# An encoder trunk on one core: elementwise work behind the first stage moves from GpSimd to VectorE

## The chip, the cores and the metric

One core of a Trainium2 chip runs the whole program. The metric is the device time of one execution in microseconds, the median over several runs. The core has five engines with queues of their own that work side by side and signal each other by semaphores: TensorE (PE in the profile; its weight loads are PEld), VectorE (DVE), ScalarE (ACT), GpSimd (POOL) and SyncE (SP, which here only issues loads and stores).

## The reference

A trunk of two layers over 256 tokens of width 2048, all in float32. Layer 0 mixes tokens with a bidirectional S5 state-space model and a gated linear unit, layer 1 with windowed grouped-query attention; each is followed by an MLP with a squared ReLU, 8192 wide.

```python
for i in range(DEPTH):                      # DEPTH = 2
    if i % 2 == 0:
        h = h + s5_mixer(rms_norm(h, s5_norm[j]), ...)      # ends: (z @ w_glu_a) * sigmoid(z @ w_glu_b)
    else:
        h = h + windowed_gqa(rms_norm(h, attn_norm[j]), positions, ...)
    h = h + sqrelu_mlp(rms_norm(h, mlp_norm[i]), mlp_w_up[i], mlp_w_down[i])

# windowed_gqa: 32 query heads, 4 key heads of 64; q and k get a norm per head and a rotation
x1, x2 = x[..., :half], x[..., half:]
concatenate([x1 * cos - x2 * sin, x2 * cos + x1 * sin])
# softmax over |i-j| <= 128 with a sink logit per head, then @ w_o
# sqrelu_mlp: square(relu(h @ w_up)) @ w_down
```

## The kernel before

**Precision.** Each factor of a large product is held as a rounded high part (fp32r) and the rest, its low part, and three products are summed: high by high, low by high, high by low (`mm3`, lines 717 to 719; the MLP has its own forms at lines 858, 860 and 924). So every weight tile must be split before TensorE can use it.

**Weights.** `wload` fetches the next tile of a fixed list, `wsrc`: a load on SP's queue into a ring of raw buffers (line 674), a copy on ScalarE that rounds to the high part (line 679), a subtraction that gives the low part (line 680). A table `whow` says for a tile into how many pieces these two are cut and which engine subtracts: "v" is one whole tile of 128x2048 on VectorE, "vv" two halves there, "g" one whole tile on GpSimd, "gggg" four quarters there. The constant `QH` gives this for the 20 tiles of the attention's projections (four for keys and values, then four for each of the four groups of heads), `UH` for the first five tiles of the first up projection, `OH` for the output projection. Every other tile is "v", apart from those of the first stage that a range `WP` gives to GpSimd, and those of the down projection that `wload_fast` splits (lines 693 to 698).

**Stages, in order of time.** The S5 stage with tables, scan and output, beside which the gated unit's first half runs (to some 290 us; GpSimd works through most of it). The rest of the gated unit (`glu_rest`, to some 394 us): per block of 512 columns and half of the tokens, `glu_post` multiplies by the sigmoid, adds to the residual (lines 816 to 823) and calls `norm_pre`, which multiplies the residual by the norm's gain (line 735) and squares it on ScalarE; `norm_post` transposes that product on TensorE and splits it (lines 744 to 747). Then the first MLP (up projection to 751 us, down projection to some 1097 us), whose end takes four norm products for attention through `scaled`. Then attention: keys and values, then four groups of eight heads each, whose projection by TensorE is set between the softmax steps of the group before. Per group and half of the tokens: `head_r` makes the head norms (lines 1095 to 1101, with the reciprocal square root at lines 199 to 208), `rope` the rotation by two products and a sum (lines 1086 to 1088), then come scores with a running maximum (line 1134), exponentials on ScalarE (line 1149), the division (line 1153), transposes (1159) and the product with the values (1168). Keys go through `rope` too, and two copies on GpSimd (line 1230). The output projection ends with residual sums and norm products for the second MLP (`fin`, line 1267), to some 1389 us. The second MLP is like the first, without norm products.

**Order.** Each engine takes its instructions in the order of its own queue. That order is not the order of the source: the program is built with `TileContext(nc, schedule_with_timeline_sim=True)`, which plans the queues by a simulated timeline. A few orders are fixed by hand with `issue_after`. The attention's steps are set between TensorE's tiles by the table `HS`.

Of the kernel before, what the change touches and what calls it, by code (L numbers as in the profile page):

```python
# [35 lines left out]
WP = range(9, 33)  # L36
WD = 20 + 16 + 64 + 64
FAST = (range(2, 27, 3), (0, 4, 7, 10, 13, 16, 20, 23, 26))
QH = ("v", "vv", "vv", "v") + ("vv", "g") * 8
UH = ("vv", "vv", "gggg", "vv", "vv")  # L40
OH = ("v",) * 16


# [134 lines left out]
class Kernel:  # L178
# [549 lines left out]
        self.nc.sync.dma_start(gain, self.gain_src[:, cb * 512:(cb + 1) * 512])  # L728
        return gain

    def norm_pre(self, cb, tt, gain, hg, e=None):

        nc = self.nc
        r = self.resid[:, tt, cb * 512:(cb + 1) * 512]
        (e or nc.gpsimd).tensor_mul(hg, r, gain)
        sq = self.tmp.tile([P, 512], F32, name="sq")
        nc.scalar.activation(sq, r, AF.Square, accum_out=self.ss[:, tt, cb:cb + 1])

# [105 lines left out]
    def mlp(self, nxt, fin):  # L844
        nc, ar = self.nc, self.ar
# [53 lines left out]
        v = nc.vector  # L899
        aform, atail = [], []  # L900

        def split(kp, fast, own=False):
            h = hTs[0][:, 2 * kp:2 * kp + 2] if kp < 16 else hTs[kp // 8 - 1][:, kp % 8 * 2:kp % 8 * 2 + 2]
            h = h.rearrange("p k c -> p (k c)")
            a = (atail if own else aform)[kp % 2]
            n = a.shape[1] // 2
            if fast:
                s = pool.tile([P, 7 * P], F32, name="sr", bufs=1)
                q = h.rearrange("p (x c) -> p x c", x=4)
                t = s.rearrange("p (x c) -> p x c", x=7)  # L910
                nc.scalar.copy(s[:, :3 * P], h[:, P:])
                v.tensor_add(t[:, 3:5], q[:, 1:4:2], q[:, 0:1].broadcast_to([P, 2, P]))
                v.tensor_add(t[:, 5], t[:, 4], q[:, 1])
                v.tensor_add(t[:, 6], t[:, 5], q[:, 2])
                h = s
            c = h.shape[1]
            nc.scalar.copy(a[:, :c], h)  # L917
            v.tensor_sub(a[:, n:n + c], h, a[:, :c].bitcast(F32))  # L918
            return a[:, :n], a[:, n:]
# [14 lines left out]
        def fast(a, w, first, end):  # L934
            for bk, j, g, c in LATE if first else FORMS:
                mm(bk, a, j, w[g], c, stop=end and bk[0] != "x")

        def plain(a, w, bk, stop=False):
            t, j = divmod(bk, 2)
            bk = "x%d" % (bk + 1)  # L940
            for i in range(2):
                mm(bk, a, (1, 0, 2, 3)[2 * i + t], w, (2, 3)[i] if j == 0 else i, stop=stop and i == 1)
# [4 lines left out]
        def fold():  # L947
            c, d, u, w = (self.tmp.tile([P, 512], F32, name=n) for n in ("hg", "hg", "sq", "gain"))
            g = nc.gpsimd
            nc.scalar.copy(c, bks["p1"])  # L950
            g.dma_start(rs(0, 0), c, accum_op=ALU.add)  # L951
            v.tensor_sub(u, c, bks["q6"])
            v.tensor_sub(w, u, bks["q5"])
            g.dma_start(rs(0, 1), w, accum_op=ALU.add)
            v.tensor_sub(u, bks["q7"], u)
            g.dma_start(rs(1, 0), u, accum_op=ALU.add)
            v.tensor_add(d, u, bks["q5"])
            g.dma_start(rs(1, 1), d, accum_op=ALU.add)

        def end(half, t, j):  # L960
            cb = half * 2 + j
            cs = slice(cb * 512, (cb + 1) * 512)
            v.tensor_add(self.resid[:, t, cs], self.resid[:, t, cs], bks["x%d" % (2 * t + j + 1)])
            if last:
                nc.sync.dma_start(self.d["out"][:, t, cs], self.resid[:, t, cs])
            elif half:
                scaled(t, cb, nc.gpsimd)
                if j:
                    self.norm_end(t)

        def scaled(t, cb, e):
            self.norm_pre(cb, t, gains[:, cb * 512:(cb + 1) * 512], hx[:, t, cb], e)

        atail += [ar.get("at#%d" % i, [1024], F32R, at=49664 + 1024 * i) for i in range(2)]
        nx = split(0, False, True)
# [7 lines left out]
        for half in range(2):  # L983
            bks, begun = {}, set()
            pend = []
            for kp in range(NK):
                a = nx
                if half == 0 and kp == 2:
                    ar.free("at")
                    self.wr[0].add(ar.get("wx#49664", [2048], at=49664))  # L990
                if half and kp == NK - 4:
                    for r in self.wr:
                        r.drop()
                    ar.free("wx")
                    atail[:] = [ar.get("at#%d" % i, [1024], F32R, at=49664 + 1024 * i) for i in range(2)]
                if kp + 1 < NK:
                    nx = split(kp + 1, kp + 1 in FAST[half], kp == 0 if not half else kp + 1 >= NK - 2)
                elif not half:
                    nx = split(0, 0 in FAST[1])
                w = self.wnext() if half or kp else w0  # L1000
                if half and kp == 19 and not last:
                    ar.free("hT#0")
                    hx = ar.get("hx", [2, 4, 512], at=31744)
                    gains = ar.get("hg", [D], at=35840)
                    nc.sync.dma_start(gains, self.d["gains"][nxt])
                    self.ss = self.small.tile([P, 2, 4], F32, name="ss")
                    for t in range(2):
                        for cb in range(2):
                            scaled(t, cb, v)
                if kp in FAST[half]:  # L1010
                    fast(a, w, not begun, kp == FAST[half][-1])
                    if kp == FAST[half][-1]:
                        fold()
                elif kp < NK - 1 - half:
                    for b in range(4):
                        plain(a, w, b)
                else:
                    pend.append((a, w))
            if half:
                ar.free("hT", "af")  # L1020
                if not last:
                    self.act = ar.get("act", [KT, 2, L], F32R, at=23552)
            n = half and not last
            for t in range(2):
                for p in pend[:n]:
                    for j in range(2):
                        plain(*p, 2 * t + j)
                for j in range(2):
                    for p in pend[n:]:
                        plain(*p, 2 * t + j, stop=p is pend[-1])  # L1030
                    end(half, t, j)
# [46 lines left out]
    def rope(self, pool, src, n, x, tt):  # L1078

        v = self.nc.vector  # L1080
        t1 = pool.tile([P, n, 2, 32], F32, name="rp_a") if n == 8 else self.tmp.tile([P, n, 2, 32], F32, name="gain")
        t2 = pool.tile([P, n, 2, 32], F32, name="rp_b", bufs=1) if n == 8 else self.tmp.tile([P, n, 2, 32], F32, name="sq")
        sv = src.rearrange("p (n s c) -> p n s c", n=n, s=2)
        A = self.ropeA[:, x, tt].rearrange("p (o s c) -> p o s c", o=1, s=2).broadcast_to([P, n, 2, 32])
        B = self.ropeB[:, x, tt].rearrange("p (o s c) -> p o s c", o=1, s=2).broadcast_to([P, n, 2, 32])
        v.tensor_mul(t1, sv, A)
        v.tensor_mul(t2, sv[:, :, ::-1], B)
        self.nc.gpsimd.tensor_add(t1, t1, t2)
        return t1.rearrange("p n s c -> p (n s c)")

    def head_r(self, pool, src, n, tt, scale, name):
# [194 lines left out]
    def run(self):  # L1286
        nc, d, ar = self.nc, self.d, self.ar
        self.wq = []
        self.whow = {**{163 - j: h for j, h in enumerate(QH)}, **{143 - j: h for j, h in enumerate(OH)}, **{291 - j: h for j, h in enumerate(UH)}}
        self.wsrc = ([d["wge"][c, k] for c in (1, 2, 3, 0) for k in range(KT // 2)] + [None] + [d["wgl"][c, k] for c in range(4) for k in range(KT // 4)]  # L1290
# [219 lines left out]
```

## Time and profile before

| | us |
|---|---|
| median of three runs (lowest, highest) | 2092.61 (2088.96, 2093.38) |
| the profiled execution | 2089.93 |
| its span, first to last instruction | 2088.1 |
| busy: TensorE, VectorE, ScalarE, GpSimd | 2013.2, 1476.5, 1091.0, 338.5 |

In the profile's rows a name as L680 is a line of the kernel, `slot` is any buffer of the big arena, `bank` any of the eight banks in which TensorE leaves results. A shape as 128x512 is partitions by elements of each. A wait is named by the line that waited and by what released it last.

### The profile page before, as it was taken

The numbers are of one execution on the slowest core, as the hardware profiler recorded it, in microseconds if no ns is written. First come the engines' busy times: TensorE is split into PE (matmuls) and PEld (weight loads), VectorE is DVE, ScalarE is ACT, GpSimd is POOL, SyncE is SP. The second block draws the span as 40 slices with busy tenths as digits, with TensorE's granted clock in tenths as the row PEclk, the third lists the DMA queues.
The fourth block names the chain that finished last, engine by engine and source line by source line (L and its number), as shares of the span: only waits on it lengthen the run. The fifth ranks groups of instructions, "written<-read, shape, count | busy, mean of one in ns | idle before, by whom it ended". The sixth has DMA issues, their size and how long they took to land.

```text
span 2088.1 us, 33141 instructions
## 1 busy us (share of the span) xinstructions
PE 2013.2 (96%) x13736; PEld 1693.2 (81%) x13736; DVE 1476.5 (71%) x2096; ACT 1091.0 (52%) x1314; POOL 338.5 (16%) x260
## 2 busy tenths in 40 slices
PE   5989999899999999999999889999999999999999
PEld 4877778788888888878787667888888888787887
DVE  8899636755555578988886877465555557898886
ACT  5553645444444455655554556454444445565553
POOL 6988721200000000000022430100000000000000
PEclk9999999999999999999999999999999999999999
DMA  3224455455555555465564332455555555547554
GB/s 120 71 98 145 153 194 200 166 197 187 196 182 193 191 196 207 181 222 207 198 206 172 121 121 81 149 186 200 193 190 184 197 185 198 204 182 241 182 205 158
DMA packets 61990, 368.47 MB, mean 176 GB/s; under 512 B 7072, under 2 KB 9408, under 8 KB 21904
## 3 DMA queue, kind: packets, MB, share of 16 engines
q1 hardware_dynamic: 54144, 342.32, 46.0%
q10 hardware_dynamic: 5184, 19.49, 2.7%
q0 software_dynamic: 2512, 4.56, 1.2%
q8 instruction: 107, 1.75, 0.3%
q14 instruction: 43, 0.35, 0.0%
HBM read 360.05 MB, written 2.10 MB: 173 GB/s over the span
## 4 chain that ended last, share of the span: by engine, by line
PE 62%; DVE 9%; DMA 7%; ACT 3%; issue 2%; POOL 0%; SPq 0%; ACTq 0%; DVEq 0%
PE bank L858 22%; PE bank L924 22%; PE bank L860 12%; DMA slot<-in_wdn 4%; DVE slot L680 4%; PE bank L717 2%; PE bank L718 1%; PE bank L719 1%; ACT slot L679 1%; DVE slot L694 1%; ACT slot L693 1%; DMA slot<-in_wup 1%; DMA slot<-in_wo 1%; ACT slot L1149 1%; PE bank L1168 1%
## 5 line engine op out<-in xcount | busy, mean ns | idle before, releaser
L680 DVE TENSOR_TENSOR slot<-slot,slot 128x2048 fp32r<-128x2048 f32 (+1 forms) x285 | 628.8, 2209 | 417.2 <-ACT slot L679 414.6
L679 ACT CAST slot<-slot 128x2048 fp32r<-128x2048 f32 (+2 forms) x321 | 554.6, 1733 | 466.5 <-PE bank L858 195.1
L924 PE MATMUL bank<-slot,slot 128*128 128x512 f32 x2124 | 493.4, 390 | 2.5 <-DVE slot L918 1.8
L858 PE MATMUL bank<-slot,slot 128*128 128x512 f32 x2048 | 492.4, 392 | 2.8 <-DVE slot L747 1.6
L924 PEld LDWEIGHTS bank<-slot,slot 128*128 128x128 f32 x2124 | 397.7, 188 | 88.4 <-DVE slot L918 4.2
L858 PEld LDWEIGHTS bank<-slot,slot 128*128 128x128 f32 x2048 | 377.0, 189 | 76.5 <-DVE slot L747 2.2
L860 PEld LDWEIGHTS bank<-slot,slot 128*128 128x128 f32 x2048 | 263.1, 191 | 10.3
L860 PE MATMUL bank<-slot,slot 128*128 128x256 f32 x2048 | 266.3, 283 | 0.0
L717 PE MATMUL bank<-slot,slot 128*128 128x512 f32 x544 | 219.2, 404 | 5.2 <-ACT slot L679 4.9
L719 PE MATMUL bank<-slot,slot 128*128 128x512 f32 x544 | 209.5, 398 | 7.3 <-POOL slot L680 7.1
L718 PE MATMUL bank<-slot,slot 128*128 128x512 f32 x544 | 215.5, 396 | 0.0
L924 PE MATMUL bank<-slot 128*128 128x512 f32 x840 | 201.1, 391 | 4.1 <-DVE slot L918 3.4
L951 POOL DMA_DIRECT2D slot<-slot x4 | 3.7, 921 | 1159.0 <-ACT slot L950 1149.3
L924 PEld LDWEIGHTS bank<-slot 128*128 128x128 f32 x840 | 157.0, 188 | 40.2 <-DVE slot L918 6.5
L694 DVE TENSOR_TENSOR slot<-slot,slot 128x1536 fp32r<-128x1536 f32 x72 | 145.5, 2021 | 39.5 <-ACT slot L693 36.4
L693 ACT CAST slot<-slot 128x1536 fp32r<-128x1536 f32 x72 | 122.3, 1698 | 93.3 <-DMA slot<-in_wdn 46.5
L869 ACT ACTIVATE slot<-slot 128x256 f32<-128x256 f32 x128 | 52.8, 414 | 159.0 <-DVE slot L867 159.0
L717 PEld LDWEIGHTS bank<-slot,slot 128*128 128x128 f32 x544 | 104.0, 191 | 30.0 <-ACT slot L679 6.1
L719 PEld LDWEIGHTS bank<-slot,slot 128*128 128x128 f32 x544 | 102.8, 191 | 31.4 <-POOL slot L680 9.1
L718 PEld LDWEIGHTS bank<-slot,slot 128*128 128x128 f32 x544 | 103.9, 191 | 20.8 <-issue 0.7
L917 ACT CAST slot<-slot 128x512 fp32r<-128x512 f32 (+1 forms) x128 | 90.5, 709 | 53.5 <-PE bank L924 52.9
L680 POOL TENSOR_TENSOR slot<-slot,slot 128x1024 fp32r<-128x1024 f32 (+2 forms) x36 | 100.6, 2808 | 104.6 <-ACT slot L679 98.9
(238 smaller groups left out, 1800.0 us busy)
## 6 DMA issues: line engine op xcount, KB each, us to landing
slot<-in_wup SPq DMA_DIRECT2D x128, 1024.0 KB, 4.9
slot<-in_wdn SPq DMA_DIRECT2D x128, 1024.0 KB, 4.9
slot<-in_wqkv SPq DMA_DIRECT2D x20, 1024.0 KB, 5.0
slot<-in_wge ACTq DMA_DIRECT2D x32, 512.0 KB, 3.8
slot<-in_wgl SPq DMA_DIRECT2D x16, 1024.0 KB, 5.3
slot<-in_wo SPq DMA_DIRECT2D x16, 1024.0 KB, 4.9
slot<-in_bz SPq DMA_DIRECT2D x16, 336.0 KB, 3.3
slot<-in_cp SPq DMA_DIRECT2D x16, 256.0 KB, 2.7
```

The lines of the kernel that those rows point to most:

```text
L679: self.nc.scalar.copy(hi[:, c], raw[:, c])
L680: (self.nc.gpsimd if e == "g" else self.nc.vector).tensor_sub(lo[:, c], raw[:, c], hi[:, c].bitcast(F32))
L693: self.nc.scalar.copy(hi, x)
L694: v.tensor_sub(lo, x, hi.bitcast(F32))
L717: pe.matmul(out, lhsT=xh, rhs=wh, start=first, stop=False)
L718: pe.matmul(out, lhsT=xl, rhs=wh, start=False, stop=False)
L719: pe.matmul(out, lhsT=xh, rhs=wl, start=False, stop=last)
L858: pe.matmul(bk, lhsT=wh[:, kt], rhs=act[:, kt].rearrange("p x c -> p (x c)"), start=(kt == 0), stop=False)
L860: pe.matmul(bk[:, :L], lhsT=wl[:, kt], rhs=act[:, kt, 0], start=False, stop=(kt == KT - 1))
L869: nc.scalar.activation(o if fb % 2 else o[:, ::-1], s.rearrange("p (x c) -> p x c", x=2), AF.Square)
L917: nc.scalar.copy(a[:, :c], h)
L924: pe.matmul(bank(bk), lhsT=a[x][:, j], rhs=w[y][:, c], start=bk not in begun, stop=stop and y == 1)
```

## The change

Three things that GpSimd does behind the first stage are done by VectorE:

- the low parts of weights: eight tiles of the heads' projections, which were whole tiles on GpSimd, become whole tiles on VectorE (`QH`); the third tile of the first up projection goes from four quarters on GpSimd to two halves on VectorE, and its rounding copies on ScalarE from four to two (`UH`);
- the products of residual and gain in `norm_pre`: eight in the gated unit, four at the end of the first down projection (`end`, second half) and eight in attention's `fin`; the four that `scaled` does in the middle of the down projection were VectorE's before;
- the sum that ends a rotation in `rope`: eight for the heads, two for the keys.

GpSimd keeps the first stage's work, the key copies of line 1230 and the DMAs that it issues.

```diff
-QH = ("v", "vv", "vv", "v") + ("vv", "g") * 8
-UH = ("vv", "vv", "gggg", "vv", "vv")
+QH = ("v", "vv", "vv", "v") + ("vv", "v") * 8
+UH = ("vv", "vv", "vv", "vv", "vv")
...
-    def norm_pre(self, cb, tt, gain, hg, e=None):
+    def norm_pre(self, cb, tt, gain, hg):
...
-        (e or nc.gpsimd).tensor_mul(hg, r, gain)
+        nc.vector.tensor_mul(hg, r, gain)
...
             elif half:
-                scaled(t, cb, nc.gpsimd)
+                scaled(t, cb)
...
-        def scaled(t, cb, e):
-            self.norm_pre(cb, t, gains[:, cb * 512:(cb + 1) * 512], hx[:, t, cb], e)
+        def scaled(t, cb):
+            self.norm_pre(cb, t, gains[:, cb * 512:(cb + 1) * 512], hx[:, t, cb])
...
-                            scaled(t, cb, v)
+                            scaled(t, cb)
...
-        self.nc.gpsimd.tensor_add(t1, t1, t2)
+        v.tensor_add(t1, t1, t2)
```

## The prediction

> **What bounds the kernel now.** I read the page's head first, then the sums by stretch, then TensorE's own waits, then the chain of waits in the stretches where TensorE stands still, and last the timeline of GpSimd beside that chain.
>
> ```profile
> span 2088.1 us, 33141 instructions
> PE 2013.2 (96%) x13736; PEld 1693.2 (81%) x13736; DVE 1476.5 (71%) x2096; ACT 1091.0 (52%) x1314; POOL 338.5 (16%) x260
> ```
>
> TensorE is busy for 96% of the span, so a change on other engines can only win where TensorE is not fed. The next view says where that is (per engine: busy us and number of instructions; then the granted TensorE clock, the DMA share and GB/s).
>
> ```profile
> core 0: us, PE busy (x) PEld busy (x) DVE busy (x) ACT busy (x) POOL busy (x), PEclk, DMA share, GB/s
> 345.00:400.00 55.00, 50.87 (x236) 41.73 (x235) 40.01 (x51) 27.33 (x37) 18.03 (x10) 0.97 0.50 177
> 1040.00:1100.00 60.00, 60.00 (x282) 50.01 (x281) 49.84 (x85) 35.73 (x42) 11.40 (x13) 1.00 0.57 182
> 1130.00:1180.00 50.00, 43.23 (x201) 33.37 (x201) 38.39 (x93) 22.04 (x39) 21.44 (x10) 0.93 0.33 118
> 1180.00:1230.00 50.00, 42.32 (x258) 31.80 (x256) 37.85 (x102) 30.33 (x62) 17.98 (x5) 0.94 0.33 126
> 1230.00:1280.00 50.00, 47.37 (x278) 36.33 (x276) 37.57 (x117) 28.89 (x66) 12.70 (x5) 0.92 0.30 106
> 1335.00:1400.00 65.00, 63.79 (x315) 53.32 (x314) 37.87 (x50) 31.08 (x34) 11.11 (x7) 1.00 0.49 170
> 1400.00:1742.00 342.00, 342.00 (x1971) 302.43 (x1970) 190.85 (x191) 161.45 (x190) 0.00 (x0) 1.00 0.55 192
> ```
>
> Behind the first stage GpSimd works in just the stretches where TensorE idles. In 1130 to 1280, the heads of attention, TensorE idles 6.8 + 7.7 + 2.6 = 17.1 us of 150, and its granted clock there is 0.93, 0.94 and 0.92: 7%, 6% and 8% of 50 us, 10.5 us of lost speed at most. At the turn from the gated unit to the first up projection (345 to 400) it idles 4.1 us at clock 0.97, 1.7 us more. Between 1400 and 1742 it is busy for 342.00 us of 342: what is saved earlier is not waited away there. So at most 17.1 + 10.5 + 4.1 + 1.7 + 1.2 (1335 to 1400), some 35 us, can be won.
>
> What ends TensorE's waits, in 1100 to 1400 and then in 300 to 410 (total, times, longest):
>
> ```profile
> PE bank L1168 <- DVE mx L1134: 4.7, 1, 4.7
> PE bank L719 <- POOL slot L680: 4.1, 3, 2.0
> PE bank L1159 <- DVE slot L1153: 4.0, 2, 2.5
> PE bank L717 <- ACT slot L679: 3.5, 1, 3.5
> ```
>
> ```profile
> PE bank L744 <- POOL slot L735: 3.9, 1, 3.9
> ```
>
> Two of the five name GpSimd (a weight subtraction, a norm product), two VectorE's softmax, one the scalar engine's weight copy. Why VectorE is late is in the chain of waits (start, length, piece): its longest pieces between 1118 and 1225, set beside two rows of GpSimd's timeline:
>
> ```profile
> 1119.64 3.58 DVE hms L1098
> 1133.55 5.59 DVE slot L680
> 1139.16 4.99 DMA slot<-in_wqkv
> 1150.83 4.46 DVE rs_h L200
> ...
> 1184.81 1.92 DVE slot L1153 x7
> 1189.65 3.72 DVE slot L680
> 1193.81 6.81 DMA slot<-in_wqkv
> 1204.01 4.30 DVE slot L680
> 1217.53 6.47 DVE slot L1153 x8
> ```
>
> ```profile
> 1118.57 4.62 POOL L680 TENSOR_TENSOR slot<-slot,slot 128x2048 fp32r<-128x2048 f32 x1 [22.50 <-ACT slot L679]
> ```
>
> ```profile
> 1150.67 4.58 POOL L680 TENSOR_TENSOR slot<-slot,slot 128x2048 fp32r<-128x2048 f32 x1
> ```
>
> L1098 and L200 work on a few numbers per partition, yet take 3.58 and 4.46 us. They end at 1123.22 and 1155.29; GpSimd's subtractions end at 1123.19 and 1155.25. VectorE stood still until GpSimd was done. Undisturbed, the same forms take (groups by shape of 1180 to 1230 and 1230 to 1285; count, busy us, mean ns):
>
> ```profile
> L200 DVE TENSOR_SCALAR rs_h<-hms 128x8 f32<-128x8 f32 x2 | 0.3, 161 | 0.0
> ```
>
> ```profile
> L680 DVE TENSOR_TENSOR slot<-slot,slot 128x1024 fp32r<-128x1024 f32 x1 | 1.2, 1216 | 0.0
> ```
>
> Seven instructions of L1153 take 1.92 us in the chain's own row at 1184.81, 0.27 each; the eight at 1217.53 take 6.47.
>
> So the chain holds stalls of 3.4 (L1098, taken at L200's 0.16), 5.59 - 1.22 = 4.4, 4.46 - 0.16 = 4.3, 3.72 - 1.22 = 2.5, 4.30 - 1.22 = 3.1 and 6.47 - 8 x 0.27 = 4.3: 22.0 us in which the chain waits for GpSimd without naming it.
>
> **The change part by part.** The durations, by groups of one shape: GpSimd's costliest of 300 to 1400, then VectorE's two nearest.
>
> ```profile
> L680 POOL TENSOR_TENSOR slot<-slot,slot 128x2048 fp32r<-128x2048 f32 x8 | 38.5, 4811 | 66.2 <-ACT slot L679 66.2
> L735 POOL TENSOR_TENSOR slot<-slot 128x512 f32<-128x512 f32 x16 | 28.0, 1757 | 173.2 <-DVE slot L1267 62.9 <-issue 58.3 <-DVE slot L823 33.3
> L1088 POOL TENSOR_TENSOR slot<-slot,slot 128x512 f32<-128x512 f32 x8 | 15.2, 1900 | 48.6 <-DVE slot L1087 28.0 <-DVE hms L1098 17.1 <-DVE slot L208 2.5
> L735 POOL TENSOR_TENSOR slot<-slot,slot 128x512 f32<-128x512 f32 x4 | 5.1, 1290 | 16.1 <-DVE slot L963 16.0
> L680 POOL TENSOR_TENSOR slot<-slot,slot 128x512 fp32r<-128x512 f32 x4 | 5.0, 1291 | 8.2 <-ACT slot L679 8.2
> ```
>
> ```profile
> L680 DVE TENSOR_TENSOR slot<-slot,slot 128x2048 fp32r<-128x2048 f32 x249 | 571.3, 2296 | 400.8 <-ACT slot L679 400.5
> ```
>
> ```profile
> L735 DVE TENSOR_TENSOR slot<-slot,slot 128x512 f32<-128x512 f32 x4 | 2.5, 684 | 0.0
> ```
>
> *The heads' weights (QH).* Eight of the projection's tiles change from "g" to "v": GpSimd loses 8 x 4.81 = 38.5 us, VectorE gains 8 x 2.30 = 18.4. By code a tile is still one copy on the scalar engine, one subtraction and one load on SP's queue; the next load into its raw buffer, and what stands behind it on SP's queue, waits for the subtraction, now in VectorE's queue. The chain shows what that wait is worth: a 4.99 us load starts at 1139.16, as a stalled subtraction ends, a 6.81 us load at 1193.81 behind another. *The rotation sums (L1088).* Eight of 128x512 and two of half that go to VectorE. It shows no sum of this form with four dimensions; the nearest row is its own 128x512 product from two buffers, 0.68 us, the farthest GpSimd's own 1.90. I take 0.68, since that row is of the same engine and size: 8 x 0.68 + 2 x 0.34 = 6.1 (bounds 0, if they fit into idle time, and 17.1). Moved work in attention: 18.4 + 6.1 = 24.5 us, against 22.0 us of stalls on the chain alone. VectorE's load is about the same; but what was a 4.6 us block at any moment becomes 2.3 us in queue order, and the tile is ready 2.5 us sooner.
>
> What TensorE gets of it. The three waits for L680 on GpSimd, 4.1 us, go: the subtraction is half as long, and VectorE idles some 12 us of each 50 there. Bounds: all 4.1, or none if the tile queues for 2 us behind other VectorE work; I take 4.1. The 4.7 us wait at L1168 stands behind the 6.47 us run of L1153, which held a 4.3 us stall; the subtraction that made it now stands somewhere in VectorE's queue for 2.3: I take 4.3 - 2.3 = 2.0 (bounds 0 and 4.7). The other two, 4.0 + 3.5, end in the softmax: VectorE's stalls ahead of them go, the moved work comes, and the scalar engine's exponentials between remain. I take half, 3.7 (bounds a loss of 2.5, 24.5 - 22.0, and a gain of 7.5). Together 9.8 of the 16.3 us in these four rows, or 60%. What is late next there is the exponentials.
>
> The clock falls with the waits. I take the same 60% of 10.5: 6.3 us (bounds 0 and 10.5). In 1230 to 1280 the longest wait in the rows is the 2.5 us of L1159, and the clock is 0.92 all the same: waits that are only shortened to some 2 us can still cost it. The Trainium skill ("TensorE: Matmul & The Clock Gate", What's actually happening) puts the fall to half speed behind at least one idle window of about 3.4 us; what that would make of the sum is rival 4, and the 2.5 us wait beside 0.92 speaks against it.
>
> *The turn into the up projection (UH, norm products of the gated unit).* Tile 2's subtractions go from four of 1.29 on GpSimd to two of 1.22 on VectorE, its copies from four to two. Eight products of L735 follow, of 20 in all. Timeline rows:
>
> ```profile
> 389.86 1.68 DVE L822 TENSOR_TENSOR slot<-slot,slot 128x512 f32<-128x512 f32 x1
> ```
>
> ```profile
> 392.35 1.77 POOL L735 TENSOR_TENSOR slot<-slot 128x512 f32<-128x512 f32 x1 [1.35 <-DVE slot L823]
> ```
>
> L822 is 1.0 over the 0.68 of its size and ends with GpSimd's subtraction; the product, on the chain, goes from 1.77 to 0.68, 1.1 less. Against these 2.1 us stand up to 2.4 of subtractions ahead of the chain. VectorE idles 15 us of this stretch of 55, so I take half, 1.2: a gain of 0.9 (bounds a loss of 2.4 and a gain of 5.8, all idle time and clock).
>
> *The other twelve products.* Four at the end of the first down projection lie where TensorE is busy 60.00 us of 60; eight at the end of attention where it is busy 63.79 of 65 and VectorE only 37.87. At 0.68 us each they are covered by TensorE's work already queued: I take 0. If that cover is gone the last two of each kind stand on the path, 4 x 0.68 = 2.7 us. GpSimd's queue keeps its key copies and its DMAs in their order, and loses only what stood between them; the moved instructions issue no DMA.
>
> Sum: 9.8 + 6.3 + 0.9 = 17.0 us off. The profiled execution took 2089.93 us for its span of 2088.1, so it would come to 2072.9; it lies 2.7 under the median of the runs, 2092.61, which gives 2075.6 for a median. I say 2076.
>
> **The rivals.** *Only the named waits go* (1). TensorE's waits for GpSimd vanish, the softmax's stay, because the exponentials and the weight copies on the scalar engine set them (the 3.5 us row ends on its copy). Against: VectorE's stalls stand in the same chain, ahead of the softmax. Then 4.1 + 0.9 and no clock, 5.0, of which up to 2 is given back as the next tile is late: 2088 to 2090, taken 2089, just inside 0.2%. That 0.2% (4 us) is about what a measurement of this kernel tells from no change.
>
> *VectorE's queue becomes the path* (2), the slower one. VectorE takes instructions in its own order, and the build plans that order by a simulated timeline that is made anew. If it sets all 24.5 us of moved work ahead of softmax and rotation, the chain wins 22.0 and pays 24.5, and the turn pays its 2.4: 4.9 slower, 2097.5. It decides from the point where more of the moved work is on the path than the stalls that left it, 22.0 in attention. For it: VectorE is busy 38 us of 50 there. Against: it idles some 12 us of each 50, and the plan need not put every moved instruction in front.
>
> *Everything goes* (3). All 16.3 us of the four rows, 10.5 of clock, 5.8 at the turn: 32.6 off, 2060. For it: without GpSimd's blocks VectorE runs at the lengths that the undisturbed rows show. Against: the weight copies behind the exponentials, 3.5 us, are the scalar engine's.
>
> *The whole clock comes back* (4). If the clock falls only behind waits longer than some 3 us, then the 4.7 and 3.5 us waits alone cost it, both are shortened, and all 10.5 return while the waits themselves give 9.8 as above: 9.8 + 10.5 + 0.9 = 21.2 off, 2071. Against: the 0.92 beside 2.5 us.
>
> **How the numbers follow.** The forecast, a gain of 8 to 26 us around 2076, 0.56; rival 4, which lies in the same span, 0.07; rival 1, 0.18, nearly half of it faster than 0.2%; rival 2, 0.12; rival 3, 0.07. Faster 0.56 + 0.07 + 0.07 + 0.08 = 0.78, same 0.10, slower 0.12. From 2066 to 2091 lie the forecast, rival 4 and rival 1; rivals 2 and 3, about 0.2, are left out.
>
> **What the changed profile would show.** Right: GpSimd's busy time falls by the groups above to some 245 us (338.5 less the five groups' 91.8 and the two half-size rotation sums), while VectorE's stays near 1476; L200, L1098 and L1153 have one length, 0.16, 0.16 and 0.28 us; no wait names L680 or L735 on GpSimd; the three stretches of attention lose 10 us of TensorE idle time and their clock rises towards 1. Wrong: VectorE busy by 20 us or more above 1476 (the stalls were not what the lengths say), new TensorE waits for L680 on VectorE of 2 us and more, or waits for L1153 as long as now. A stall that I put down to GpSimd and that stays with GpSimd idle would overturn the first step.

## The result, and the profile after

| | before | after | ratio, 95% interval |
|---|---|---|---|
| first series, medians of 4 and 4 runs (us) | 2092.99 | 2080.22 | 0.9934 [0.9912, 0.9956] |
| second series, medians of 11 and 6 runs (us) | 2091.68 | 2077.85 | 0.9934 [0.9920, 0.9949] |
| the profiled execution of the first series | 2089.93 | 2073.64 | |

The change makes the kernel 13 to 14 us faster; 2076 was said, with 2066 to 2091 as the range. The profiled execution of after is the lowest of its four, 6.6 us below their median; the second series has a profile of its own, with a span of 2076.6 us, and what differs between the two is told at the end.

The head of the page of after:

```profile
span 2071.8 us, 33106 instructions
PE 2001.0 (97%) x13736; PEld 1685.1 (81%) x13736; DVE 1474.6 (71%) x2136; ACT 1091.5 (53%) x1312; POOL 246.1 (12%) x218
```

GpSimd lost 92 us of work. VectorE took that work over in 40 more instructions and is busy no longer than before: 1474.6 us against 1476.5. The sums by stretch of after (columns as in the prediction):

```profile
345.00:400.00 55.00, 52.30 (x257) 43.78 (x256) 44.34 (x68) 27.99 (x37) 0.00 (x0) 1.00 0.51 178
...
1130.00:1180.00 50.00, 48.78 (x263) 38.52 (x262) 39.58 (x122) 29.25 (x57) 2.53 (x4) 1.00 0.49 173
1180.00:1230.00 50.00, 39.43 (x239) 30.28 (x238) 35.55 (x124) 28.45 (x59) 0.00 (x0) 0.90 0.25 85
1230.00:1280.00 50.00, 47.64 (x307) 36.82 (x307) 32.78 (x104) 28.21 (x56) 0.00 (x0) 1.00 0.31 110
```

Three of the four stretches improved, and 1180 to 1230 got worse: TensorE idles 10.6 us there instead of 7.7, and its clock is 0.90 instead of 0.94. Fixed stretches cut the stages at other places in each kernel, so the next sums, of before and then of after, run from event to event: the first up projection (first to last product of its line 858), then attention (last product of the first down projection to the first of the second up projection).

```profile
385.45:749.22 363.77, 358.24 (x2047) 315.53 (x2046) 205.98 (x229) 171.07 (x206) 8.08 (x6) 1.00 0.53 186
1093.96:1382.90 288.94, 271.69 (x1465) 214.29 (x1463) 199.32 (x478) 153.10 (x273) 69.40 (x31) 0.96 0.38 135
```

```profile
387.18:745.96 358.78, 356.07 (x2047) 314.44 (x2046) 204.84 (x230) 169.56 (x202) 0.00 (x0) 1.00 0.53 185
1091.23:1369.91 278.68, 264.35 (x1465) 210.37 (x1463) 190.46 (x504) 154.33 (x273) 2.53 (x4) 0.98 0.40 141
```

TensorE does the same products in both (2047 and 1465 records). So a shorter busy time is read as clock regained, and length less busy time is waiting. The up projection, with the turn at its head, is 5.0 us shorter: 2.8 of waiting and 2.2 of clock. Attention is 10.3 shorter: only 2.9 of waiting (17.25 to 14.33) and 7.3 of clock. These two make 15.3 of the 16.3 us between the two profiles' spans. In attention VectorE's own busy time falls from 199.3 to 190.5 although 30 us of work were added: the 24.5 us of weights and rotation sums, and 5.4 us of eight norm products that fall into this stretch (VectorE has 26 instructions more there, 8 + 10 + 8). So 39 us of standing still are gone.

TensorE's waits of after, in attention and at the turn (total, times, longest):

```profile
PE bank L1159 <- DVE slot L1153: 7.5, 1, 7.5
PE bank L1168 <- ACT slot L1161: 6.5, 4, 2.9
```

```profile
PE bank L744 <- DVE slot L735: 2.7, 1, 2.7
```

No wait there names GpSimd any more, and the 3.5 us on the scalar engine's weight copy is gone. But one wait for the softmax's division is now 7.5 us long; it is called the hole below. TensorE's timeline has it (start, length, instruction, in brackets the idle time before it), and the sums give the clock around it:

```profile
1201.68 2.00 PE L1130 MATMUL bank<-slot,slot 64*128 64x256 f32 x16 [0.21 <-ACT slot L1121]
1211.13 1.94 PE L1159 MATMUL bank<-ident,slot 128*128 128x128 f32 x8 [7.46 <-DVE slot L1153]
1215.97 1.13 PE L1168 MATMUL bank<-slot 128*64 128x128 f32 x8 [2.90 <-ACT slot L1161]
```

```profile
1208.60:1218.84 10.24, 4.81 (x25) 4.11 (x26) 8.85 (x50) 7.48 (x25) 0.00 (x0) 0.50 0.02 6
```

Between the scores (line 1130) and the transposes that need the finished softmax (line 1159) TensorE's queue holds no weight product at this place, so it stands until the softmax is done and waits again for the copy of line 1161, and the clock is at half for 10.24 us. VectorE's groups of one shape from 1080 to 1400, of before and then of after:

```profile
L680 DVE TENSOR_TENSOR slot<-slot,slot 128x1024 fp32r<-128x1024 f32 x20 | 34.2, 1720 | 9.9 <-ACT slot L679 9.8
L1153 DVE TENSOR_SCALAR slot<-slot,den 128x256 f32<-128x256 f32 x64 | 30.4, 548 | 0.2
L200 DVE TENSOR_SCALAR rs_h<-hms 128x8 f32<-128x8 f32 x8 | 7.8, 988 | 0.0
```

```profile
L680 DVE TENSOR_TENSOR slot<-slot,slot 128x2048 fp32r<-128x2048 f32 x33 | 75.5, 2289 | 57.1 <-ACT slot L679 55.2 <-PE bank L718 1.8
L680 DVE TENSOR_TENSOR slot<-slot,slot 128x1024 fp32r<-128x1024 f32 x20 | 24.2, 1219 | 2.0 <-ACT slot L679 2.0
L1153 DVE TENSOR_SCALAR slot<-slot,den 128x256 f32<-128x256 f32 x64 | 17.5, 349 | 0.1
L1088 DVE TENSOR_TENSOR slot<-slot,slot 128x512 f32<-128x512 f32 x8 | 5.5, 685 | 0.0
L200 DVE TENSOR_SCALAR rs_h<-hms 128x8 f32<-128x8 f32 x8 | 1.3, 164 | 0.0
L1098 DVE TENSOR_SCALAR hms<-hms 128x8 f32<-128x8 f32 x8 | 1.3, 162 | 0.0
```

Every form has its undisturbed length. The sum of a rotation costs 685 ns, where 0.68 us was taken from a neighbouring row.

### The profile page after: what moved, and what is told of

It reads as the page before. It is cut to its first block, busy times and chain, and to the rows that moved or that the text cites. A ratio compares the mean times of both kernels' runs of the same rounds, so it can differ in the third digit from the quotient of the medians.

```text
span 2071.8 us, 33106 instructions
## 1 busy us (share of the span) xinstructions
PE 2001.0 (97%) x13736; PEld 1685.1 (81%) x13736; DVE 1474.6 (71%) x2136; ACT 1091.5 (53%) x1312; POOL 246.1 (12%) x218
## 4 chain that ended last, share of the span: by engine, by line
PE 73%; DVE 6%; DMA 3%; issue 2%; ACT 2%; DVEq 0%; ACTq 0%
PE bank L858 22%; PE bank L924 22%; PE bank L860 12%; PE bank L719 5%; PE bank L717 5%; PE bank L718 5%; DMA slot<-in_wdn 3%; DVE slot L680 3%; DVE slot L694 1%; PE bank L1168 1%; ACT slot L693 1%; PE bank L1159 1%; DVE slot L918 1%; PE bank L1130 1%; ACT slot L679 0%
## 5 line engine op out<-in xcount | busy, mean ns | idle before, releaser
L680 DVE TENSOR_TENSOR slot<-slot,slot 128x2048 fp32r<-128x2048 f32 (+1 forms) x295 | 638.8, 2168 | 414.7 <-ACT slot L679 412.2
L679 ACT CAST slot<-slot 128x2048 fp32r<-128x2048 f32 (+1 forms) x319 | 554.5, 1743 | 465.2 <-PE bank L858 190.3
L860 PEld LDWEIGHTS bank<-slot,slot 128*128 128x128 f32 x2048 | 263.1, 191 | 10.3
L717 PE MATMUL bank<-slot,slot 128*128 128x512 f32 x544 | 216.8, 400 | 1.1 <-ACT slot L679 0.8
L717 PEld LDWEIGHTS bank<-slot,slot 128*128 128x128 f32 x544 | 102.8, 189 | 25.4 <-issue 2.1
L718 PEld LDWEIGHTS bank<-slot,slot 128*128 128x128 f32 x544 | 102.7, 189 | 20.6 <-issue 0.5
L918 DVE TENSOR_TENSOR slot<-slot,slot 128x512 fp32r<-128x512 f32 (+1 forms) x128 | 101.8, 798 | 1.7 <-ACT slot L917 0.8
```

The lines of the kernel that those rows point to most:

```text
L679: self.nc.scalar.copy(hi[:, c], raw[:, c])
L680: (self.nc.gpsimd if e == "g" else self.nc.vector).tensor_sub(lo[:, c], raw[:, c], hi[:, c].bitcast(F32))
L717: pe.matmul(out, lhsT=xh, rhs=wh, start=first, stop=False)
L718: pe.matmul(out, lhsT=xl, rhs=wh, start=False, stop=False)
L860: pe.matmul(bk[:, :L], lhsT=wl[:, kt], rhs=act[:, kt, 0], start=False, stop=(kt == KT - 1))
```

## The experiments

Each ran beside the kernel before on its chip; ratios are to that. The theory is that GpSimd's reads hold VectorE up, and that the gain is the end of that. Three questions were open: whether it is that at all, why attention's waiting barely shrank, and what gave 5 us at the turn.

### The eight weight tiles alone

Before, with one line changed:

```diff
-QH = ("v", "vv", "vv", "v") + ("vv", "g") * 8
+QH = ("v", "vv", "vv", "v") + ("vv", "v") * 8
```

> Only the weights of the heads move to VectorE (QH); norm products, rotation sums and the third up tile stay on GpSimd. Theory (GpSimd's blocks of VectorE and its slow subtractions made the heads late): most of the gain between the last down product of the first MLP and the first up product of the second stays, 7 to 11 us of the 10.3 that the profiles of before and after differ there, and the turn into the first up projection stays as before: 2082 to 2086 in all. Rival (the planner's new order did it, and it needs the rotation sums on VectorE too): attention gains under 4 us, 2088 to 2093.

Measured 2076.27 us, 0.9928 [0.9913, 0.9942], better than the theory's 2082 to 2086. Attention in its profile, and its longest wait:

```profile
1096.55:1370.07 273.52, 264.02 (x1464) 209.50 (x1463) 186.52 (x486) 153.49 (x272) 30.99 (x23) 0.99 0.41 143
```

```profile
PE bank L1159 <- DVE slot L1153: 7.1, 1, 7.1
```

Attention is 15.4 us shorter than before, 7.75 of it waiting (17.25 to 9.50) and 7.7 clock; the whole change took only 10.3 there. So the eight tiles carry attention's gain, and something else in the change gives a third of it back. The waiting that went is that of the rows for weights and rotation (4.1 at line 719, 3.5 at line 717, 0.3 at line 1119); TensorE's waits for the softmax and behind it, 9.1 us in before, still sum to 9.0.

### The turn and the norm products alone

Before, with the changes of `UH` and of all norm products, but `QH` and the rotation sums left on GpSimd.

> Only the third up tile and the norm products move (UH, norm_pre); the heads' weights and rotation sums stay on GpSimd. Theory: the turn into the first up projection gets its 3 to 5 us (one wait of TensorE shorter, no half-clock stretch at 395 us), attention stays as before within 2 us: 2087 to 2090. Rival (the norm products alone carry the gain of attention, by its end): 2084 or less.

Measured 2087.52 us, 0.9975 [0.9964, 0.9986], as expected. Attention is 288.8 us long, as in before; the first up projection 358.8, as in after. The two parts act in different stages, and their gains, 4.4 and 15.6 us by medians, sum to 20; the whole change gives 13 to 14. The rotation sums are in neither part.

### GpSimd's reads put back beside the moved work

After, with two GpSimd subtractions of 128x1024 per moved tile into a buffer that nobody reads (VectorE still makes the low parts):

```diff
+def beside(k, how, hi):            # called by wload for the eight tiles, "d" in QH
+    for _ in range(2 * (how == "d")):
+        k.nc.gpsimd.tensor_sub(k.dm, hi[:, :1024].bitcast(F32), hi[:, 1024:].bitcast(F32))
```

TensorE, VectorE, the scalar engine and SP have the same instructions in the same order as in after.

> The changed kernel, with 8 x 2 subtractions of 128x1024 added on GpSimd that read the high part of each of the eight moved tiles and write a buffer that nobody reads. The order of the instructions on TensorE, VectorE, ScalarE and SyncE is the same as without them. Theory (a block: VectorE's instructions from buffers stand still while GpSimd works on buffers): VectorE's busy time rises by 15 to 35 us, L200, L1098 or L1153 become long again, and the kernel loses 5 to 12 us against the changed one: 2085 to 2092. Rival (the moved subtraction was late, and that is all; or the plan's order did it): as the changed kernel, 2078 to 2082.

Measured 2098.62 us, 1.0034 [1.0022, 1.0045]: 18 to 21 us above after, and slower than before. The rows: GpSimd's added group, two of VectorE's, attention.

```profile
L1514 POOL TENSOR_TENSOR slot<-slot 128x1024 f32<-128x1024 f32 x16 | 49.5, 3092 | 123.3 <-ACT slot L679 122.7
```

```profile
L680 DVE TENSOR_TENSOR slot<-slot,slot 128x1024 fp32r<-128x1024 f32 x20 | 29.4, 1480 | 0.8 <-ACT slot L679 0.8
L1153 DVE TENSOR_SCALAR slot<-slot,den 128x256 f32<-128x256 f32 x64 | 26.1, 483 | 0.1
```

```profile
1092.33:1392.42 300.09, 275.64 (x1464) 216.17 (x1463) 213.37 (x504) 154.14 (x273) 52.69 (x20) 0.94 0.37 131
```

Work whose result nobody uses makes VectorE's busy time in attention 22.9 us longer (213.37 against 190.46) and the stage 21.4 longer. VectorE's instructions are the same, so the lengths are GpSimd's doing, and TensorE pays for nearly all of it: 10.1 us of waiting (24.45 against 14.33) and 11.3 of clock. The mechanism is as told; its price was expected at 5 to 12 us and is more than half as much again as the upper end.

### The same, with GpSimd writing and hardly reading

```diff
-        k.nc.gpsimd.tensor_sub(k.dm, hi[:, :1024].bitcast(F32), hi[:, 1024:].bitcast(F32))   # twice
+        k.nc.gpsimd.tensor_copy(k.dm[:, :8], hi[:, :8].bitcast(F32))
+        for _ in range(5):
+            k.nc.gpsimd.memset(k.dm, 0.0)
```

> As the kernel before it in this list, but GpSimd reads only 8 elements and then fills the buffer five times (128x1024 each), so that it works about as long and nearly only writes. Theory of a block by reading: subtractions and products from two buffers (L680, L1088) keep their lengths, and the kernel stays within 2 us of the changed one, 2078 to 2082, unless one-input instructions (L200, L1098, L1153) are held by writes too; then those alone lengthen, and 2082 to 2087. Rival (any GpSimd work on buffers holds VectorE alike): as with reads, 2085 to 2092.

Measured 2081.51 us, 0.9956 [0.9942, 0.9971], within what after shows. GpSimd's added groups, and VectorE's two:

```profile
L1516 POOL MEMSET slot<- 128x1024 f32 x40 | 38.5, 962 | 2.3
L1514 POOL COPY slot<-slot 128x8 f32<-128x8 f32 x8 | 14.1, 1760 | 109.6 <-ACT slot L679 109.6
```

```profile
L680 DVE TENSOR_TENSOR slot<-slot,slot 128x1024 fp32r<-128x1024 f32 x20 | 24.2, 1219 | 0.6 <-ACT slot L679 0.5
L1153 DVE TENSOR_SCALAR slot<-slot,den 128x256 f32<-128x256 f32 x64 | 20.6, 396 | 0.1
```

GpSimd is occupied for 52.6 us, about as long as in the run above (38.5 of it writing), and the time hardly moves. VectorE's two-input subtraction keeps its 1219 ns beside GpSimd's writes: eight of the twenty begin while a memset runs, and none takes more than 1.23 us. In the run above, three that begin well inside a GpSimd subtraction take 2.8 to 3.1 us. So for the two-input subtraction it is the reading. The one-input division is held by writes too (20.6 us against 17.5): the four that begin during a memset take 1.11 to 1.13 us instead of 0.35 and end 0.1 to 0.2 us behind it. They cost less than in the run above at least in part because a memset is shorter, 962 ns against 3092. The Trainium skill ("SBUF — State Buffer", Who interferes with whom) states just this split: a VectorE instruction with two inputs in that memory contends with a GpSimd instruction that reads, one in a two-port mode with any, and the one that starts first keeps the ports for its whole length. Both runs agree with it; that the division works in such a mode no run here shows.

### The change without the rotation sums

After, with line 1088 on GpSimd as before:

```diff
-        v.tensor_add(t1, t1, t2)
+        self.nc.gpsimd.tensor_add(t1, t1, t2)
```

> The changed kernel with the rotation sums alone back on GpSimd. Attention gained 15.4 us when only the weights moved and 10.3 with the whole change, by the profiles. Theory (the rotation sums cost attention some 5 us, by the place that the plan gives them or the instructions behind them, and the gain at the turn adds to the rest): 2070 to 2074. Rival (the rest of the difference is the norm products' or one profile's luck): as the changed kernel, 2077 to 2082.

Measured 2072.93 us, 0.9913 [0.9899, 0.9926], as expected: 5 to 7 us better than the whole change, and near the sum of the two parts. TensorE's waits in attention:

```profile
PE bank L1159 <- DVE slot L1153: 7.1, 1, 7.1
PE bank L1168 <- ACT slot L1161: 1.9, 2, 1.2
```

The 7 us hole is there all the same; the waits behind it at L1168 are 1.9 us instead of 6.5. Is it the sums' price on VectorE, or the order of the queues, which the build plans anew (TensorE's queue differs from after's at many places)? The three runs with `HS` below tell.

### The softmax steps set two positions earlier

`HS` says behind how many steps of the projection each part of attention stands. Two positions earlier for the turn of the queries and the scores with their softmax; transposes and products stay:

```diff
-HS = ((0, 5, 6, 7, 12, 13, 14, 15, 16), (1, 9, 10, 11, 19, 20, 21, 22, 23))
+HS = ((0, 3, 4, 5, 12, 13, 14, 15, 16), (1, 7, 8, 9, 19, 20, 21, 22, 23))
```

In before:

> The kernel before with another table HS: scores two steps sooner in the attention of a group, all else as before. The plan then has weight products between the scores and the transposes behind the softmax in more places. Theory (GpSimd's blocks make the heads late whatever the order): gains at most 5 us, 2086 to 2093. Rival (the order is what the change won by): 2078 to 2084.

Measured 2087.01 us, 0.9977 [0.9968, 0.9987], as the theory has it. In after:

> The changed kernel with the same other table HS. In its profile one wait of 7.5 us and one of 2.9 at half clock stand where the plan has no weight product between scores and transposes; the new table puts at least ten there. Theory (that hole is what the change leaves): 8 to 13 us less than the changed kernel, 2067 to 2073. Rival (the softmax sets the pace and the hole moves elsewhere): within 4 us of it, 2077 to 2083.

Measured 2067.07 us, 0.9883 [0.9870, 0.9897]: the fastest version of all, 24 us under before and 11 to 13 under the change. Its waits in attention are one row, beside the stage's sum:

```profile
PE bank L1168 <- ACT slot L1161: 4.5, 3, 2.1
```

```profile
1091.44:1359.83 268.39, 263.87 (x1465) 208.78 (x1463) 189.58 (x504) 153.07 (x273) 3.15 (x4) 0.99 0.42 146
```

With weight products between scores and transposes the hole is gone: attention waits 4.5 us in place of 14.3. In before the same spacing gives only 4.3 us; GpSimd's blocks remain there (VectorE's 128x1024 subtractions take 1660 ns on average, against 1219). And with line 1088 on GpSimd once more:

> The other table HS and the whole change, but the rotation sums back on GpSimd. With the old table that won 4 us in attention over the whole change. Theory (the sums cost nothing by themselves; with the old table they moved weight products out of the hole): with the new table no gain, and the plan here has one weight product only between scores and transposes at one place, so 2067 to 2073. Rival (six microseconds more in VectorE's queue are on the path): 2062 to 2065.

Measured 2069.22 us, 0.9889 [0.9876, 0.9903], no faster than with the sums on VectorE. So the sums show no price of their own, and what they spoiled in the change was, as far as these runs tell, the order that the build then chose. It is not shown outright, since this plan is a new one too, with waits for the softmax of its own:

```profile
PE bank L1159 <- DVE slot L1153: 4.4, 2, 3.6
```

### The turn: the tile or the products

Before with only `UH` changed:

> The kernel before with the third up tile alone moved (UH). Theory (at the turn the block of L822 by GpSimd's subtraction, 1.0 us, and the slow product, 1.1 us, count each by itself, and the half clock goes only if the wait gets short enough): the first up projection's stage shrinks by 1 to 2 us from 363.8, 2089 to 2092 in all. Rival (the tile was the whole cause): it shrinks by 4 to 5 us, 2086 to 2088. Rival (the product was): no change, 2091 to 2093.

Measured 2093.13 us, 1.0009 [1.0000, 1.0018], no gain: the theory missed. Before with only the twenty norm products moved:

> The kernel before with the twenty norm products alone moved to VectorE; the third up tile alone gave nothing, both together 5.0 us in the stage of the first up projection (363.8 to 358.8). Theory (the slow product on the chain was the cause and the tile's block second): that stage shrinks by 2 to 4 us, 2088 to 2091 in all. Rival (only both together bring the wait under the length at which the clock falls): under 1.5 us, 2090 to 2093. Rival (the tile is of no use): the whole 4 to 5 us, 2086 to 2088.

Measured 2085.41 us, 0.9965 [0.9953, 0.9977], better than the theory; it is the last rival, that the tile is of no use. The waits at the turn, of the tile alone and then of the products alone:

```profile
PE bank L744 <- POOL slot L735: 4.4, 1, 4.4
PE bank L858 <- DVE slot L747: 1.3, 1, 1.3
```

```profile
PE bank L858 <- DVE slot L747: 1.7, 1, 1.7
PE bank L719 <- DVE slot L680: 0.2, 1, 0.2
```

The first up projection is 364.3 us long with the tile and 358.1 with the products, against 363.8 and 358.8 for before and after. The tile is worth nothing: with it on VectorE, subtractions of half a tile stand in the chain ahead of the product (one of 1.23 us right ahead of lines 817 and 747), where the subtraction on GpSimd had lengthened line 822. The norm products were the whole gain: with them alone on VectorE the wait of 3.9 us at line 744 is not there, and one of 1.7 us at line 858 remains. With both moved, as in after, 2.7 us remain at line 744.

### The first stage's subtractions too

The version with the new `HS`, and `WP = range(9, 9)`: the first stage's 24 subtractions of 128x1024 also go to VectorE.

> The other table HS and the whole change, and the 24 weight subtractions of the first stage moved to VectorE as well (WP empty). Theory (a block costs only where VectorE's late work holds TensorE): the last gated-unit product comes at some 387 us in every profile, the scan and the copies of VectorE fill that stage, 24 x 1.2 us more there; between 4 us faster and 6 slower than the new table alone, 2063 to 2073. Rival (blocks by GpSimd are as dear there): 2055 to 2062.

Measured 2068.83 us, 0.9882 [0.9868, 0.9897], the same as without. GpSimd's busy time falls to 190.8 us. VectorE's rises from 1473.7 to 1488.6, by 14.9 us for 24 x 1.22 = 29.3 us of work, so some 14 us of standing still went here as well, without any gain in time. The first up projection begins at 390.0 us instead of 386.8; in the profiles in which these subtractions stayed on GpSimd it begins at 385.2 to 390.0, so no difference is to be seen. What a block costs there and what the subtractions cost VectorE, no run takes apart.

### The change itself once more

> The changed kernel itself once more, in five rounds, because its four executions so far lie apart (2073.64, then 2079.99 to 2081.28) and the difference to the version that moves the eight weight tiles alone (2076.27) is no larger than that. Theory: the hole that the new order of attention leaves (7.5 and 2.9 us at half clock) is there in every execution, so the time is 2078 to 2082, some 4 us above the version with the tiles alone, in spite of the 5 us that the turn saves. Rival: the 2073.64 is the typical one, the hole costs little, and the time is 2072 to 2075, below the tiles alone.

Measured 2077.85 us (2075.56 to 2079.86), 0.9934 [0.9920, 0.9949], between the two; the hole is there with the same lengths. Against the tiles alone (2076.27) it is level within both intervals: the turn's 5 us are about what the new order gives back in attention (273.5 us long with the tiles alone, 278.7 and 281.2 in the two profiles of the change).

## Why the prediction was right, point by point

**First step, that VectorE stands still while GpSimd works.** Right, and shown: the lengths fell to those foretold (L200 and L1098 at 0.16 us, L1153 at 17.5 / 64 = 0.27), GpSimd came to 246.1 for 245 and VectorE to 1474.6 for 1476, and the reads put back bring the stalls and the time back in the same order of instructions. The 22.0 us on the chain were a part; 39 us left VectorE in attention. This is also why rival 2, VectorE's queue as the path, fell: the stalls that went were more than the 30 us that came. The 1476 itself was not worked out: all moved work is 40.5 us by the prediction's lengths (18.4 + 6.1 + 20 x 0.68 + 2.4), and less the 22.0 it would have made 1495. That it came true needed nearly twice the stalls that were counted. And not all of the gain is of this kind: the 4.1 us at line 719 were waits for GpSimd's own subtraction, which takes 4.81 us where VectorE needs 2.30. No run takes these two parts of the gain in time apart.

**The waits, 9.8 us.** This is the step that failed. The term of 4.1 us for L680 on GpSimd held, and the 3.5 us at L717, of which half was taken, is gone whole. But 2.0 and half of 4.0 were taken off the softmax's waits, and these went from 4.7 + 4.0 to 7.5 + 6.5. Attention's waiting shrank by 2.9 us, and the foretold 10 us less idle time in its three stretches did not come. The sign "waits for L1153 as long as now" was put down as proof against the theory; it came, longer, and the theory holds: L1153 itself ran undisturbed, but TensorE's queue had no product to do meanwhile. That the order is planned anew stood in rival 2 only as a way to put work in front of the path. That it also decides what TensorE has left to cover the softmax was missed. With the tiles alone the waits lose 7.75, near the 9.8, but by the rows for weights and rotation; those of the softmax are as long as before. With the better spacing the waits lose 12.7. In size rival 1's 4.1 us of waits was nearer to the 2.9 than the forecast. Its reason fails all the same: the 3.5 us on the weight copy went, and the softmax's waits stayed for want of a product in TensorE's queue, since with the other `HS` they are gone at line 1159.

**The clock, 6.3 us.** Right: 7.3 in the first profile, 4.8 in the second (busy 266.92). Rival 4, that all of it returns, did not happen, since one long hole remained.

**The turn, 0.9 us within -2.4 and 5.8.** Mis-sized: it gave 5.0. The product was counted as 1.1 us shorter, and half of the added subtractions against it. But 2.8 us of waiting went (3.9 and 1.6 became one wait of 2.7), and the clock with it (2.2 of the 5.0 us are clock). The tile's edit, counted as part of the gain, gives nothing.

**The twelve other products, 0.** No loss is to be seen; TensorE's busy time in the stretches that hold them is 60.00 us of 60 and 64.94 of 65.

So the sum, 17.0 against 16.3 between the two profiles, came out because an overestimate in attention's waits (6.9 too much) met an underestimate at the turn (4.1 too little) and a clock term that was 1.0 low. That the errors nearly cancel is luck. So is the profile: the first one is the lowest of its four executions. The second one's span is 11.5 us shorter than before's, and the medians give 13 to 14, so the 17.0 was 3 to 4 us too much. Rival 1 was too small in all since it gave nothing for the clock and no more than the forecast for the turn. Rival 3, 2060, came within 7 us once the steps were spaced anew; the change alone could not give it.

## What to carry to other kernels

Before giving elementwise work to an engine that seems free, read the lengths of the other engine's smallest instructions beside it: a 128x8 operation of 4.46 us that ends when GpSimd's subtraction ends tells more than a wait that names GpSimd. Here eight subtractions on GpSimd cost VectorE 31 us (199.3 + 18.4 - 186.5, with the tiles alone), more than the 18.4 us in which it does them itself. And when a build plans its queues anew, judge a moved instruction by the new order too: look for places where TensorE has nothing between producing and consuming a softmax, and set the steps again, since that was worth nearly as much as the move (11 to 13 us, but only 4.3 in the kernel before).

## What the runs showed of the hardware that was not expected

**The block goes both ways.** In the run that mainly writes, GpSimd's copy of eight elements per partition took 1760 ns on average, nearly twice a memset of 1024 elements (962). Where it met one of VectorE's 2.29 us subtractions it took 2.24 to 2.31 us (six times), elsewhere 0.26 and 0.30.

**The clock differs between executions with the same waits.** The second profile of after has the same hole (7.47 and 2.90 us), and then a wait that the first one has as well. Rows of the first and of the second profile, TensorE's timeline:

```profile
1256.61 0.67 PE L1168 MATMUL bank<-slot 128*64 128x128 f32 x8 [2.06 <-ACT slot L1161]
```

```profile
1257.74 0.66 PE L1168 MATMUL bank<-slot 128*64 128x128 f32 x8 [2.06 <-ACT slot L1161]
```

The sums behind that wait in the first, and around hole and wait in the second, with attention's own:

```profile
1256.60:1262.00 5.40, 5.39 (x38) 4.15 (x38) 5.40 (x7) 1.62 (x3) 0.00 (x0) 1.00 0.51 184
```

```profile
1207.40:1221.05 13.65, 6.82 (x29) 5.72 (x30) 11.12 (x63) 8.87 (x30) 0.00 (x0) 0.50 0.12 50
1258.60:1262.01 3.41, 3.41 (x14) 2.93 (x12) 3.41 (x6) 0.59 (x1) 0.00 (x0) 0.50 0.50 149
```

```profile
1091.41:1372.66 281.25, 266.92 (x1466) 212.37 (x1463) 190.34 (x504) 154.54 (x273) 2.53 (x4) 0.97 0.39 139
```

After a wait of 2.06 us the clock stayed at 1.00 in one execution and fell to 0.50 for 3.41 us in the other; behind the hole it was low for 10.24 and for 13.65 us, three and four times 3.41. That is 2.6 us of attention between two executions of one program. The Trainium skill ("TensorE: Matmul & The Clock Gate", What's actually happening) describes a window of 3413 ns that runs on its own and does not start anew with the kernel, and the multiples and the difference agree with it. Its figure of at least one idle window before the clock falls is more than was needed here: 2.06 us sufficed, and in before a wait of 1.99 us that ended at 1138.11, behind which the clock was 0.50 from 1138.83 to 1142.24.
